# The load and store queue of a streaming encoder layer takes its order from the kernel's own planner

## The chip, the cores and the metric

The kernel runs on one core of a Trainium2 chip. The metric is the device time of one execution in microseconds (us). TensorE (PE in the profile) does the matmuls, VectorE (DVE), ScalarE (ACT) and GpSimd (POOL) the rest, and SyncE (SP) issues all DMAs.

## The reference, cut to what matters

One step of an encoder layer for 2048 new positions (prompt) and 64 further positions of a running stream (sample, with 4096 cached positions). All is float32.

```
h = rmsnorm(x, norm_g) @ w_in                  # 1024 -> 6144 columns
qa, ka, va, za, qb, kb, vb, zb, ga, gb = split(h)
# branch A: differential attention, 4 heads, two 64-wide halves c, 128-wide values
s = qa . ka / 8 - slope[h] * |q_pos - k_pos|,  masked by chunks of 64
a = softmax(s[c=0]) - lam * softmax(s[c=1]);   oa = a @ va
# branch B: retention with a running state r per head
s = (qb . kb) * d_intra;   ob = s @ vb + (qb * xi) @ r;   r = decay * r + (kb * zeta)^T @ vb
# output
oa = rmsnorm(oa) * silu(za);   ob = rmsnorm(ob) * silu(zb)
m = sigmoid(ga) * (oa @ w_oa) + sigmoid(gb) * (ob @ w_ob)
y = x + m @ w_out
```

The outputs are y, the normalised keys and values (k, v) of prompt and sample, and the retention states.

## The kernel before

Every large product is done as three matmuls on a high and a low part of each operand (hi*hi, hi*lo, lo*hi), so weights and inputs are split on ScalarE and on VectorE or GpSimd before they are used (`w_split`, `split_fin`).

The projection (`w_stream`) runs over the two halves of the prompt (1024 rows each, the sample with the first) and, within a half, over column groups of `w_in`. `natural` makes q, k, v and vb with rows on the partitions; `transposed` makes the others with columns on the partitions. A group's result leaves PSUM in a finishing task (`fin_qk`, `fin_va`, `fin_vb`, `fin_t`) that copies it to SBUF and stores it to scratch tensors in DRAM (`qT`, `kT`, `vN`, `vbN`, `qbT`, `kbT`, `zaT`, `zbT`, `gaT`, `gbT`). The buffers are few: one `thi`, two `tlo`, three `ev` (with `raw`).

The second stream (`z_stream`) runs beside it: for each half, attention over four heads. `load_head` fetches K and V of a head, `load_q` the queries of a pair of 128-row blocks, `qk_block` and `softmax` make the weights, `at_pv` multiplies with V and stores the normalised result to `oaT` from the one buffer `r_o`. After the first half come `sample_attn` and the retention (`ret_sample`, `ret_some`, `ret_block`), which stores to `obT`.

When the projection is done its pool is closed and the memory is used again for the output stage: `out_prep` loads w_oa and w_ob (`wst` in the buffers `oz`), o and z of each group of 264 columns, `load_wout` loads w_out, `gate` loads the gates (`gt`); `m_tile` and `m_fin` make m, `y_tile` and `y_fin` make y.

The order of the work comes from a planner inside the kernel. Each task is a Python generator; `loop` always advances the runnable task of the highest priority and emits its instructions as it goes. `P`, `A`, `V`, `G` add planned durations to clocks of the engines, `take` and `give` hand buffers out with the time at which they are believed free, and a `yield t` means "not before t on PE's clock". A DMA has a planned cost too:

```
    def ld(self, dst, src, nbytes=0):
        self.nc.sync.dma_start(dst, src)
        self.dma = max(self.dma, self.pe) + nbytes / 300.0
        return self.dma + DMA_LAT          # 2600 ns

    st = ld
```

The emitted order is binding only for the engines that `MANUAL` names: PE, ScalarE and VectorE. For SP and GpSimd the framework's scheduler chooses the order by its own estimate. All waits are semaphores that the framework derives from the data; an engine's queue works in order, so an instruction that waits holds back those behind it. Some loads are paced by the plan alone: x tiles by `XFLY` (three in flight in the first half, five in the second), the loads of a head until 9 us after the mark of its q, k and v.

Of the kernel before, what the change touches and what calls it, by code (L numbers as in the profile page):

```python
# [16 lines left out]
T = 2048  # L17
# [17 lines left out]
        "mm": 2, "s": 2, "at": 2, "pv": 1, "tp": 1,  # L35
        "oz": 11, "og": 16, "gt": 6, "wst": 4, "m": 18, "xt": 2, "yt": 2}
LAT = 250.0
DMA_LAT = 2600.0
QUANT = 6

# [16 lines left out]
class Hybrid:  # L57
# [449 lines left out]
    def fin_qk(self, which, g, nh=2):  # L507
        nc = self.nc
        ep = self.ep
        hs = slice(2 * g, 2 * g + nh)  # L510

        def fin(ps, r, nu, t0, t):
            n, ng, rt = 128 * nh * nu, 2 * nh * nu, r * nu
            yield from self.take("ev")
            yield from self.take("tlo")
            raw = self.sb(ep, [128, 512], "ev", "raw")[:r, :n]
            sq = self.sb(ep, [128, 512], "tlo", "sq")[:r, :n]
            ms = self.sp.tile([128, 8], F32, tag="ms", name="ms")[:r, :ng]
            raw3 = raw.rearrange("p (g d) -> p g d", d=64)
            nc.scalar.activation(sq, ps, AF.Square)  # L520
            t1 = self.A(n, t)
            if which == "q":
                nc.scalar.copy(raw, ps)
                t2 = self.A(n, t)
            else:
                nc.vector.tensor_mul(raw3, ps.rearrange("p (g d) -> p g d", d=64),
                                     self.gk[:r].unsqueeze(1).to_broadcast([r, ng, 64]))
                t2 = self.V(n, t)
            self.give("mm", max(t1, t2))
            yield t1  # L530
            nc.vector.tensor_reduce(ms, sq.rearrange("p (g d) -> p g d", d=64),
                                    axis=AX.X, op=ALU.add)
            t = self.V(n, t1)
            self.give("tlo", t)
            if which == "q":
                nc.vector.scalar_tensor_tensor(out=ms, in0=ms, scalar=64.0 * EPS,
                                               in1=self.qinv[:r, 2 if nh == 4 else g, :ng], op0=ALU.add, op1=ALU.mult)
            else:
                nc.vector.tensor_scalar(ms, ms, 1.0 / 64, EPS, op0=ALU.mult, op1=ALU.add)
            t = self.V(8)  # L540
            yield t
            rs = yield from self.rsqrt_small(ms, ng, t)
            nc.vector.tensor_mul(raw3, raw3, rs.unsqueeze(2).to_broadcast([r, ng, 64]))
            t = self.V(n)
            yield t
            ts = 0
            if which == "k":
                if t0 < T:
                    dst = self.o["k_prompt"][0, 0, t0:t0 + rt, hs]
                else:  # L550
                    dst = self.o["k_sample"][0, 0, :, hs]
                ts = self.rows_out(dst.rearrange("t h c d -> t (h c d)"), raw, nu, nh << 16)
            yield from self.take("tp")
            tp = self.psum("tp")
            for u in range(nu):
                for h in range(nh):
                    c = 128 * (nh * u + h)
                    nc.tensor.transpose(tp[:, h * rt + u * r:h * rt + u * r + r], raw[:, c:c + 128],
                                        self.ident[:r, :r])
                    t = self.P(256)  # L560
            self.give("ev", max(t, ts))
            yield from self.take("thi")
            yield from self.take("tlo")
            hi = self.sb(ep, [128, 512], "thi", dt=F32R)[:, :nh * rt]
            lo = self.sb(ep, [128, 512], "tlo", dt=F32R)[:, :nh * rt]
            pt = tp[:, :nh * rt]
            if which == "q":
                nc.scalar.activation(hi, pt, AF.Identity, scale=self.gq)
                nc.vector.scalar_tensor_tensor(out=lo, in0=pt, scalar=self.gq, in1=hi.bitcast(F32),
                                               op0=ALU.mult, op1=ALU.subtract)  # L570
                dst = self.qT
            else:
                nc.scalar.copy(hi, pt)
                nc.vector.tensor_sub(lo, pt, hi.bitcast(F32))
                dst = self.kT
            t1 = self.A(n, t, 40)
            t2 = self.V(n, t1)
            self.give("tp", t2)
            for d, s, tag, w in zip(dst, (hi, lo), ("thi", "tlo"), (t1, t2)):
                if w > self.pe:  # L580
                    yield w
                self.give(tag, self.st(d[hs, :, t0:t0 + rt].rearrange("h p t -> p h t"),
                                       s.bitcast(F32).rearrange("p (h t) -> p h t", h=nh), nh * nu << 16))

        return fin

    def fin_va(self, g, nh=2):
        nc = self.nc
        ep = self.ep
        hs = slice(2 * g, 2 * g + nh)  # L590

        def fin(ps, r, nu, t0, t):
            n, rt = 128 * nh * nu, r * nu
            yield from self.take("ev")
            yield from self.take("thi")
            yield from self.take("tlo")
            raw = self.sb(ep, [128, 512], "ev", "raw")[:r, :n]
            hi = self.sb(ep, [128, 512], "thi", dt=F32R)[:r, :n]
            lo = self.sb(ep, [128, 512], "tlo", dt=F32R)[:r, :n]
            nc.scalar.copy(hi, ps)  # L600
            t1 = self.A(n, t)
            nc.scalar.copy(raw, ps)
            t2 = self.A(n, t)
            nc.vector.tensor_sub(lo, ps, hi.bitcast(F32))  # L604
            t3 = self.V(n, t1)
            self.give("mm", max(t2, t3))
            if t0 < T:
                dst = self.o["v_prompt"][0, 0, t0:t0 + rt, hs]
            else:
                dst = self.o["v_sample"][0, 0, :, hs]  # L610
            yield t1
            gsl = slice(256 * g, 256 * g + 128 * nh)
            self.give("thi", self.rows_out(self.vN[0][t0:t0 + rt, gsl], hi.bitcast(F32), nu, nh << 16))
            yield t2
            td = self.rows_out(dst.rearrange("t h e -> t (h e)"), raw, nu, nh << 16)
            if t0 == T:
                td = self.st(self.vsN[:, gsl], raw, 1 << 16)
            self.give("ev", td)
            yield t3
            self.give("tlo", self.rows_out(self.vN[1][t0:t0 + rt, gsl], lo.bitcast(F32), nu, nh << 16))  # L620

        return fin

    def fin_vb(self, g):
        nc = self.nc
        ep = self.ep

        def fin(ps, r, nu, t0, t):
            n, rt = 256 * nu, r * nu
            yield from self.take("ev")  # L630
            raw = self.sb(ep, [128, 512], "ev", "raw")[:r, :n]
            nc.scalar.copy(raw, ps)
            t = self.A(n, t)
            self.give("mm", t)
            yield t
            self.give("ev", self.rows_out(self.vbN[t0:t0 + rt, 256 * g:256 * g + 256], raw, nu, 1 << 17))

        return fin
# [17 lines left out]
    def fin_t(self, ps, n, dst, t0, scale, grouped, t):  # L656
        nc = self.nc
        yield from self.take("ev")
        ev = self.sb(self.ep, [128, 512], "ev")[:, :n]
        if scale is None:  # L660
            nc.scalar.copy(ev, ps)  # L661
        else:
            nc.scalar.mul(ev, ps, scale)
        t = self.A(n, t)
        self.give("mm", t)
        yield t
        self.give("ev", self.put(dst, ev, t0, n, grouped))

    def put(self, dst, ev, t0, n, grouped):
# [233 lines left out]
    def at_pv(self, h, p, vs, tv, pair, last_pair):  # L903
# [26 lines left out]
        for kp in range(nkt // 2):  # L930
# [3 lines left out]
            w = 0  # L934
            segs = []
            for kt in (2 * kp, 2 * kp + 1):
                s0 = w
                for b in range(2):
# [4 lines left out]
                    t = self.P(256)  # L943
# [12 lines left out]
            t1 = self.A(w, t)  # L956
            nc.vector.tensor_sub(al[:, :w], at[:, :w], ah[:, :w].bitcast(F32))  # L957
            t2 = self.V(w, t1)
# [6 lines left out]
        t = done[0]  # L965
        if last_pair:
            self.give("V", t, len(vs[0]) * 2)
        o = yield from self.rms_t(pv, 256, self.gsub, t, "pv")
        self.give("r_o", self.put(self.oaT[h], o, 256 * p, 256, True))

    def sample_attn(self):
# [9 lines left out]
        for h in range(4):  # L981
# [3 lines left out]
            for j in range(2):  # L985
                nc.vector.memset(qq[j].bitcast(F32), 0.0)
                t = self.V(128)
# [35 lines left out]
            for m in range(9):  # L1023
                n = 512 if m < 8 else 64
                if m < 8:
                    yield lambda: len(self.kns) > 0
                    kn, t = self.kns.pop(0)
# [46 lines left out]
            t = self.P(512)  # L1074
        self.give("row", t, 2)
        o = yield from self.rms_t(fp, 256, self.gsub, t, "pv")
        for h in range(4):
            t = self.put(self.oaT[h], o[:, 64 * h:64 * h + 64], T, 64, True)
        self.give("r_o", t)
# [89 lines left out]
    def ret_block(self, k, t0, r, first):  # L1169
# [102 lines left out]
        nc.scalar.copy(res, tp)  # L1272
        t = self.A(4 * r, t)
        self.give("tp", t)
        yield t
        for h in range(4):
            rh = res[:, r * h:r * h + r]
            d3 = self.obT[h].rearrange("p (g c) -> p g c", c=GW)
# [244 lines left out]
    def y_fin(self, ps, xt, y, r, t):  # L1523
# [5 lines left out]
        t = self.V(512, t)  # L1529
        self.give("at", t)  # L1530
        self.give("xt", t)
        yield t
        self.give("yt", self.st(y, yt, 2048 * r))

    def out_stream(self):
# [138 lines left out]


def MANUAL(ET):
    return {ET.PE, ET.Activation, ET.DVE}


TLS = False  # L1680
# [60 lines left out]
```

## Time and profile before

| | |
|---|---|
| median of three runs | 2019.16 us (2017.9 to 2020.87) |
| the profiled execution | 2016.98 us, of which the span from first to last instruction 2015.2 us |
| mean granted TensorE clock | 0.997 |
| TensorE busy | 1991.4 us (99% of the span), 12414 matmuls |
| VectorE, ScalarE, GpSimd busy | 992.8, 956.9, 419.2 us |
| DMA | 278.8 MB on SP's queue, 46.8% of the time of the 16 DMA engines |

TensorE is the bound. The span is read in stages: to about 210 us only the projection runs; then projection and attention (or retention) share TensorE, with the second half's inputs transposed from about 810 us; the last group of the projection ends at about 1623 us and the output stage runs from there to the end. Waits of SP in the profile are times in which the head of its queue waits for a semaphore.

### The profile page before, as it was taken

Reading aid. Unit: us, or ns where it says so; the run is one execution under the profiler, and the core shown is the slowest. Engines: PE = TensorE matmul, PEld = TensorE weight load, DVE = VectorE, ACT = ScalarE, POOL = GpSimd, SP = SyncE. Lnnn points to the kernel's source line nnn. Section 1 sums busy time; section 2 is a strip of 40 time slices with the busy share of each in tenths; the row PEclk is TensorE's granted clock in tenths of the full one; section 3 lists DMA queues with packets and bytes.
Section 4 is the critical chain, followed back from the end, with each engine's and each line's share of the span. In section 5 each row is a group of like instructions: output and inputs, shape, how many; then the busy total and the mean of one; then the engine's idle time right before and its main releaser. Section 6 shows DMA issues by size and latency. Waiting matters only on the chain. (4 is left out here: it accounts for less than half of the span.)

```text
span 2015.2 us, 34341 instructions
## 1 busy us (share of the span) xinstructions
PE 1991.4 (99%) x12414; PEld 1786.1 (89%) x12414; DVE 992.8 (49%) x2659; ACT 956.9 (47%) x2096; POOL 419.2 (21%) x387
## 2 busy tenths in 40 slices
PE   8999999999999999999999999999999989999999
PEld 6778999999998999999999888888888878889997
DVE  6353575553331321546856655635653365444442
ACT  6332676654432433535666665645654544333221
POOL 2310121121112221221211111222112443222210
PEclk9999999999999999999999999999999999999999
DMA  6646464344565463563352252463234665444431
GB/s 228 195 146 171 135 168 130 101 140 144 150 182 131 135 178 104 164 198 123 112 157 87 85 158 68 124 190 95 64 92 126 202 216 159 144 146 133 140 94 58
DMA packets 330268, 280.96 MB, mean 139 GB/s; under 512 B 64689, under 2 KB 296113, under 8 KB 330098
## 3 DMA queue, kind: packets, MB, share of 16 engines
q1 hardware_dynamic: 330098, 278.77, 46.8%
q8 instruction: 98, 1.61, 0.3%
q14 instruction: 72, 0.59, 0.1%
HBM read 187.19 MB, written 91.49 MB: 138 GB/s over the span
## 5 line engine op out<-in xcount | busy, mean ns | idle before, releaser
L451 PE MATMUL mm<-xh,wh 128*128 128x512 f32 (+2 forms) x1280 | 461.1, 360 | 0.0
L451 PE MATMUL mm<-xh,wl 128*128 128x512 f32 (+2 forms) x1280 | 451.7, 353 | 0.0
L451 PE MATMUL mm<-xl,wh 128*128 128x512 f32 (+2 forms) x1280 | 450.9, 352 | 0.0
L422 POOL TENSOR_TENSOR wl<-ws,wh 128x512 fp32r<-128x512 f32 x190 | 251.9, 1338 | 912.3 <-ACT wh L415 632.2
L451 PE MATMUL mm<-wh,xh 128*128 128x256 f32 (+3 forms) x864 | 272.5, 315 | 0.3 <-DVE tlo L604 0.3
L451 PEld LDWEIGHTS mm<-xh,wl 128*128 128x128 f32 x1280 | 240.9, 188 | 31.9
L451 PEld LDWEIGHTS mm<-xh,wh 128*128 128x128 f32 x1280 | 241.2, 188 | 29.6 <-issue 0.2
L451 PEld LDWEIGHTS mm<-xl,wh 128*128 128x128 f32 x1280 | 241.5, 189 | 29.1
L451 PE MATMUL mm<-wh,xl 128*128 128x256 f32 (+3 forms) x864 | 267.2, 309 | 0.0
L451 PE MATMUL mm<-wl,xh 128*128 128x256 f32 (+3 forms) x864 | 266.9, 309 | 0.0
L661 ACT COPY ev<-mm 128x512 f32<-128x512 f32 x140 | 71.6, 511 | 238.8 <-PE mm L451 216.9
L451 PEld LDWEIGHTS mm<-wh,xh 128*128 128x128 f32 (+1 forms) x864 | 162.5, 188 | 11.0 <-PE s L836 0.4
L451 PEld LDWEIGHTS mm<-wl,xh 128*128 128x128 f32 (+1 forms) x864 | 162.7, 188 | 10.6
L451 PEld LDWEIGHTS mm<-wh,xl 128*128 128x128 f32 (+1 forms) x864 | 162.5, 188 | 10.2
L957 DVE TENSOR_TENSOR atl<-at,ath 128x512 fp32r<-128x512 f32 (+1 forms) x144 | 93.8, 660 | 139.8 <-ACT ath L955 139.8
L874 ACT ACTIVATE row<-row,a_mx 128x1024 f32<-128x1024 f32 (+7 forms) x160 | 153.6, 964 | 16.7 <-DVE a_mx L854 16.6
L844 DVE CUSTOM_DVE_ANT_0 row<-s,dfar 128x512 f32<-128x512 f32 (+2 forms) x192 | 117.9, 632 | 74.7 <-PE s L836 73.5
L415 ACT CAST wh<-ws 128x512 fp32r<-128x512 f32 x192 | 117.0, 619 | 40.7 <-PE mm L451 28.3
L955 ACT CAST ath<-at 128x512 fp32r<-128x512 f32 (+1 forms) x144 | 79.6, 563 | 99.3 <-PE at L942 96.9
L835 PE MATMUL s<-K,q 128*128 128x512 f32 (+3 forms) x320 | 120.3, 381 | 2.5 <-DVE a_acc L844 2.5
L836 PE MATMUL s<-K,q 128*128 128x512 f32 (+3 forms) x320 | 115.5, 362 | 0.7 <-DMA q<-qT 0.7
L895 DVE SCALAR_TENSOR_TENSOR row<-row,a_w 128x1024 f32<-128x1024 f32 (+4 forms) x96 | 98.1, 1032 | 26.7 <-ACT row L892 26.5
(206 smaller groups left out, 3945.5 us busy)
## 6 DMA issues: line engine op xcount, KB each, us to landing
ws<-in_w_in_dram SPq DMA_DIRECT2D x192, 256.0 KB, 3.1
q<-qT SPq DMA_DIRECT2D x128, 128.0 KB, 3.0
V<-vN SPq DMA_DIRECT2D x24, 512.0 KB, 5.5
K<-kT SPq DMA_DIRECT2D x48, 256.0 KB, 4.4
gt<-gaT SPq DMA_DIRECT2D x64, 132.0 KB, 2.1
gt<-gbT SPq DMA_DIRECT2D x64, 132.0 KB, 2.2
xt<-in_x_prompt_dram SPq DMA_DIRECT2D x16, 512.0 KB, 6.3
kn<-in_cache_k_T_dram SPq DMA_DIRECT2D x32, 256.0 KB, 3.9
```

The lines of the kernel that those rows point to most:

```text
L415: nc.scalar.copy(h, st)
L422: nc.gpsimd.tensor_sub(l, st, h.bitcast(F32))
L451: nc.tensor.matmul(ps, p, q, start=c == 0 and i == 0, stop=c == KC - 1 and i == 2)
L661: nc.scalar.copy(ev, ps)
L835: nc.tensor.matmul(ps, q1s, kk, start=True, stop=False)
L836: nc.tensor.matmul(ps, q2s, kk, start=False, stop=True)
L844: nc.vector.tensor_tensor_reduce(out=units[k0 // 1024][:, k0 % 1024:k0 % 1024 + n], in0=ps, in1=tab, scale=-SLOPES[h], scalar=3.0e38, op0= ...
L874: nc.scalar.activation(u, u, AF.Exp, bias=mx, scale=-1.0, accum_out=lp[:, k:k + 1])
L895: nc.vector.scalar_tensor_tensor(out=u0, in0=u0, scalar=w[:, 0:1], in1=u1, op0=ALU.mult, op1=ALU.add)
L955: nc.scalar.copy(ah[:, :w], at[:, :w])
L957: nc.vector.tensor_sub(al[:, :w], at[:, :w], ah[:, :w].bitcast(F32))
```

## The change

SP is added to the engines that follow the emitted order, so loads and stores go out in the order in which the planner emits them. Most stores are now emitted `STORE` = 700 ns after the planned time of their data (before: at that time), so that whatever the planner emits within these 700 ns stands ahead of them. In three places, `at_pv`, `sample_attn` and the k output in `fin_qk`, a store had followed its data at once: the first two now wait for the later of PE's and VectorE's planned clocks plus 700 ns, and the third stands behind the transposes of the same tile instead of ahead of them. The buffers of these stores are handed back by the planner with a correspondingly later time.

```
+STORE = 700.0
...
 def MANUAL(ET):
-    return {ET.PE, ET.Activation, ET.DVE}
+    return {ET.PE, ET.Activation, ET.DVE, ET.SP}
...
 # fin_qk: the k output moves from ahead of take("tp") to behind the transposes
-            ts = 0
-            if which == "k":
-                ...
-                ts = self.rows_out(dst.rearrange("t h c d -> t (h c d)"), raw, nu, nh << 16)
             yield from self.take("tp")
...
                     t = self.P(256)
+            ts = 0
+            if which == "k":
+                ...
+                ts = self.rows_out(dst.rearrange("t h c d -> t (h c d)"), raw, nu, nh << 16)
             self.give("ev", max(t, ts))
...
 # fin_qk, the hi and lo parts
-                if w > self.pe:
-                    yield w
+                if w + STORE > self.pe:
+                    yield w + STORE
...
 # fin_va: three stores;  fin_vb, fin_t, ret_block, y_fin: one wait each
-            yield t1
+            yield t1 + STORE
...
-            yield t2
+            yield t2 + STORE
...
-            yield t3
+            yield t3 + STORE
...
-        yield t
+        yield t + STORE
...
 # at_pv and sample_attn, ahead of the stores to oaT
         o = yield from self.rms_t(pv, 256, self.gsub, t, "pv")
+        yield max(self.pe, self.dve) + STORE
         self.give("r_o", self.put(self.oaT[h], o, 256 * p, 256, True))
```

More of the change, by code (lines that the diff above doesn't have):

```diff
@@ L545, in fin @@
             yield t
-            ts = 0
-            if which == "k":
[L548 to L551, printed above, removed]
-                ts = self.rows_out(dst.rearrange("t h c d -> t (h c d)"), raw, nu, nh << 16)
             yield from self.take("tp")
@@ L560, in fin @@
                     t = self.P(256)
+            ts = 0
+            if which == "k":
+                if t0 < T:
+                    dst = self.o["k_prompt"][0, 0, t0:t0 + rt, hs]
+                else:
+                    dst = self.o["k_sample"][0, 0, :, hs]
+                ts = self.rows_out(dst.rearrange("t h c d -> t (h c d)"), raw, nu, nh << 16)
             self.give("ev", max(t, ts))
@@ L665, in fin_t @@
         self.give("mm", t)
-        yield t
+        yield t + STORE
         self.give("ev", self.put(dst, ev, t0, n, grouped))
@@ L1076, in sample_attn @@
         o = yield from self.rms_t(fp, 256, self.gsub, t, "pv")
+        yield max(self.pe, self.dve) + STORE
         for h in range(4):
@@ L1274, in ret_block @@
         self.give("tp", t)
-        yield t
+        yield t + STORE
         for h in range(4):
@@ L1531, in y_fin @@
         self.give("xt", t)
-        yield t
+        yield t + STORE
         self.give("yt", self.st(y, yt, 2048 * r))
```

## The prediction

> **What bounds the kernel now.** I read the head of the page first, then the busy time by stretch, then who ended TensorE's waits, then the DMA queue's own waits and its order in time.
>
> ```profile
> span 2015.2 us, 34341 instructions
> PE 1991.4 (99%) x12414; PEld 1786.1 (89%) x12414; DVE 992.8 (49%) x2659; ACT 956.9 (47%) x2096; POOL 419.2 (21%) x387
> ```
>
> TensorE (PE) is busy for 1991.4 of 2015.2 us. Its 12414 matmuls are not touched, so only 2015.2 - 1991.4 = 23.8 us of idle time is open to an edit that reorders DMAs, plus whatever runs at a reduced clock. The next rows say where the idle time lies (first number after the stretch: its length; second: PE busy; the sixth field is the granted clock):
>
> ```profile
> 0.00:50.00 50.00, 44.37 (x198) 34.87 (x199) 31.14 (x70) 32.04 (x67) 11.99 (x13) 0.97 0.67 228
> 850.00:900.00 50.00, 49.13 (x412) 48.78 (x411) 26.85 (x59) 18.59 (x43) 10.27 (x8) 1.00 0.72 214
> 900.00:950.00 50.00, 48.91 (x375) 46.62 (x376) 29.12 (x87) 25.08 (x53) 5.14 (x4) 1.00 0.43 138
> 950.00:1000.00 50.00, 48.02 (x369) 45.97 (x368) 40.26 (x121) 33.91 (x73) 8.23 (x6) 1.00 0.31 95
> 1600.00:1650.00 50.00, 46.30 (x276) 41.71 (x275) 25.38 (x52) 21.36 (x51) 17.02 (x20) 0.97 0.61 187
> 1650.00:1700.00 50.00, 45.94 (x277) 40.74 (x277) 31.73 (x72) 20.41 (x52) 20.36 (x25) 0.97 0.59 185
> 2000.00:2016.00 16.00, 11.08 (x48) 6.21 (x46) 1.69 (x3) 0.00 (x0) 0.00 (x0) 0.99 0.23 67
> ```
>
> Idle: 5.63 us at the start, 0.87 + 1.09 + 1.98 = 3.94 us around the change of halves, 3.70 + 4.06 = 7.76 us at the switch to the output stage, 4.92 us at the very end. That is 22.25 of 23.8 us. Who ends PE's waits:
>
> ```profile
> PE at L1516 <- DVE ml L1485: 4.0, 2, 2.1
> PE tp L341 <- DVE xl L349: 3.9, 1, 3.9
> PE mm L1447 <- DVE gt L1467: 3.7, 3, 1.9
> PE s L835 <- DVE a_acc L844: 2.5, 4, 1.6
> PE tp L558 <- DVE raw L543: 1.3, 4, 0.5
> PE s L836 <- DMA q<-qT: 0.7, 1, 0.7
> ```
>
> Only one row, 0.7 us, is a load that the attention itself waits for. Everything else is VectorE being late. So the order of the loads can matter only through what makes VectorE late, and that is seen at one place, the switch at 1620 to 1665 us (chain of work, start and length of each piece):
>
> ```profile
> 1623.75 2.92 DMA gbT<-ev
> 1628.53 5.02 DMA wst<-in_w_out_dram
> 1633.58 0.63 ACT woh L1316
> 1634.23 0.69 DVE wol L1323
> ```
>
> The last store of the projection stage has to land before the output stage may reuse its memory; then w_out is loaded, split on ScalarE and VectorE, and VectorE, in program order, reaches its gate products (L1467) late. PE's waits of 3.7 and 4.0 us follow. They cost more than themselves, for the clock falls behind them:
>
> ```profile
> 1633.50:1637.00 3.50, 1.56 (x13) 1.35 (x12) 2.93 (x7) 3.25 (x7) 1.27 (x1) 0.99 1.04 386
> 1637.00:1640.30 3.30, 3.30 (x17) 3.30 (x16) 3.30 (x4) 2.43 (x6) 3.28 (x3) 0.50 0.43 131
> 1660.80:1664.20 3.40, 2.98 (x7) 2.42 (x8) 3.40 (x6) 1.02 (x3) 3.28 (x4) 0.50 0.54 165
> ```
>
> Two stretches of about 3.4 us run at a granted clock of 0.50, after a stretch with 1.56 us busy out of 3.50. Each costs about 1.7 us of work. The switch therefore holds 7.76 + 2 x 1.7 = 11.2 us.
>
> The Trainium skill (TensorE: Matmul & The Clock Gate, Part 1) says the clock halves after an idle window of about 3.4 us. The trace has the 3.4 us of half clock, but no wait of PE is that long (2.1 us at most), so here a window that is more than half idle was enough. By the page's rule, waits of about 2 us would bring no slow stretch, and the switch would hold 7.8 us; by the trace, such waits gathered in one window do.
>
> **The change, part by part.** No DMA, matmul or copy is added or removed. What moves is the order of SyncE's (SP's) queue, in which each issue holds back all behind it.
>
> *Where SP waits now.*
>
> ```profile
> SPq L132 <- POOL wl L422: 261.4, 152, 7.3
> SPq L132 <- ACT ev L661: 260.4, 85, 16.0
> SPq L132 <- DVE oyt L1528: 82.9, 23, 16.8
> ```
>
> ```profile
> 1618.32 0.38 SPq L132 DMA_DIRECT2D gbT<-ev  x1
> 1619.44 0.33 SPq L132 DMA_DIRECT2D z<-zaT  x1
> 1620.13 0.32 SPq L132 DMA_DIRECT2D on<-oaT  x1
> 1623.75 0.37 SPq L132 DMA_DIRECT2D gbT<-ev  x1
> 1624.52 0.94 SPq L132 DMA_DIRECT2D z<-zaT  x1
> 1627.59 3.93 SPq L132 DMA_DIRECT2D wst<-in_w_out_dram  x8
> ```
>
> SP stands 260.4 us in front of stores whose copy (L661) is not done, 3.1 us each time. From 1620.45 to 1623.75 it stands so with a z load behind it. Taking loads ahead of such stores is what the edit does. Its worth is bounded by what PE waits for: among PE's waits none is ended by `on` or `z`, and the 0.7 us for q is all a load delays directly. So from this part I take -0.7 us; at most the switch and the change of halves go too (rival 1).
>
> *The last gbT store at the switch.* The plan puts it 0.7 us (STORE) behind its data, and what follows it in the plan (closing the pool, w_out, the gates) moves too. On the chip SP does not wait for the plan's clock, only for order and semaphores: it reaches the store early and issues when the copy ends. Cost between 0 (SP is there first, as now) and 0.7 us plus one load in front that waits for its slot (3.1 us, the mean wait above). Nearest is the row at 1623.75, where SP waits for the store: I take 0, and keep +3.8 for the range.
>
> *The stores' later due times elsewhere.* Each due time also says when the planner believes a buffer is free, so with 0.7 us more the order on PE, ScalarE and VectorE can shift. The one buffer of `thi` is the tightest: in the plan it was held for the copy, two latencies of 0.25 us and a store of 262144/300 + 2600 ns, 0.6 + 0.5 + 3.5 = 4.6 us; now 5.3 us, against the 24 matmuls of a tile.
>
> ```profile
> 1589.79 0.39 PE L451 MATMUL mm<-xl,wh 128*128 128x512 f32 x1
> 1590.47 0.39 PE L451 MATMUL mm<-xl,wh 128*128 128x512 f32 x1
> ```
>
> These two stand three matmuls apart, 0.68/3 = 0.227 us each, so a tile takes 5.4 us. The hold still fits, with 0.1 us to spare; without that cover it would cost its excess in each tile. I take 0; either sign is possible, and I give it 4 us each way, the idle time around the change of halves (3.94), which is where such shifts now show.
>
> *Loads that stood far ahead fall back to their planned place.* The order of before runs ahead of the plan:
>
> ```profile
> 8.04 5.67 SPq L132 DMA_DIRECT2D xt<-in_x_prompt_dram  x6
> 33.87 0.43 SPq L132 DMA_DIRECT2D state<-in_state_ret_dram  x1
> ```
>
> Six x tiles are issued in a row though the plan allows three in flight (XFLY), and the retention state is fetched at 33.87 us, long before the sample's attention and the retention that follows it. Afterwards each stands where the plan has it, with the plan's latency, and that is shorter than the measured one:
>
> ```profile
> q<-qT SPq DMA_DIRECT2D x128, 128.0 KB, 3.0
> V<-vN SPq DMA_DIRECT2D x24, 512.0 KB, 5.5
> K<-kT SPq DMA_DIRECT2D x48, 256.0 KB, 4.4
> ```
>
> Plan for K: 262144/300 + 2600 ns = 3.47 us against 4.4, 0.9 late; for V 524288/300 + 2600 = 4.35 against 5.5, 1.15 late. If PE stood at each of the 8 heads for both: 8 x (0.9 + 1.15) = 16.4 us; if loads arrive before their turn, 0. The row nearest to this is q: its four loads per pair (planned 4 x 0.44 + 2.6 = 4.3 us, measured three issues more plus 3.0) are already fetched about as the plan has it, and 32 pairs cost PE 0.7 us in all. So I take 1 us and keep 16.4.
>
> [...]
>
> *The moved k store* (L548 to L552, now behind four transposes at most) is issued some tenths of a microsecond later and frees `ev` later; `ev` has three buffers, and no wait on it is among PE's rows. 0.
>
> *The end.*
>
> ```profile
> 2011.11 0.68 DVE oyt L1528
> ```
>
> The last store follows this addition with nothing else left in the queue, so its 0.7 us of planned delay is not waited for. 0.
>
> Sum: -0.7 + 0 + 0 + 1 + 0 + 0 = +0.3 us on the profiled execution, 2016.98 us (1.8 us around its span), giving 2017.3. That execution is 2.2 us below the median of 2019.16, so the median to expect is 2019.5 us.
>
> **The rivals.**
>
> *Rival 1, faster: the switch and the change of halves are relieved.* If loads no longer stand behind stores, w_out and the gates come earlier, VectorE's queue is not blocked, and the half-clock stretches vanish. Half of the switch (11.2/2 = 5.6) and half of the change of halves (3.94/2 = 2.0) give 2019.2 - 7.6 = 2011.6 us; all of both, and the 3.9 us of the start, would give 2000. For it: the 260.4 us of SP's waits. Against it: at the switch the chain begins with the store that was issued the moment its copy ended, and w_out's memory is not free before it lands; no order of the queue shortens that. The start's wait is VectorE's own order.
>
> *Rival 2, slower: K and V lose their lead.* Loads that no longer run ahead of the plan land after the time at which the plan sends PE to them: at a head's start PE stands until K or V is there. It decides once the plan's landing (3.47, 4.35 us) is the time at which PE is sent there with nothing placed between. Half of 16.4 us, and one half-clock stretch of 1.7 us, give 2019.2 + 9.9 = 2029.1 us; all of it with two stretches 2039. For it: the measured 4.4 and 5.5 us. Against it: q's 0.7 us, and that PE has projection matmuls to place between.
>
> *Rival 3, the change does not do what it says.* The old order may already be nearly the plan's: at the switch z, `on` and the gbT stores alternate as a plan would have them. Then the time is 2019.2 us. It can't be told from the forecast by time, only by the queue's order.
>
> **How the numbers follow.** Forecast and rival 3 together 0.42 (the forecast 0.32, rival 3 0.10), rival 1 0.25, rival 2 0.33; rival 2 is above rival 1 because its price has rows and rival 1's best place is held by a landing that stays. A measurement of this kernel can tell about 0.2% (4 us) from no change. The forecast's own range, with its 4 us each way and the 3.8, is 2014 to 2025, so of the 0.42 some 0.06 falls below 2015.2 and 0.07 above 2023.2: faster 0.25 + 0.06 = 0.31, same 0.29, slower 0.33 + 0.07 = 0.40. The range goes from 2009 (beyond rival 1's middle) to 2033 (beyond rival 2's).
>
> **What would show it.** Right: PE busy within 2 us of 1991.4, idle of 7 to 8 us between 1600 and 1700 with the same two slow stretches, SP's wait on L661 well below 260 us, state's load just ahead of the sample's retention. Rival 1 shows as granted clock 1.00 in those two stretches and less wait on L1467 and L1485. Rival 2 shows as new rows of PE waiting on DMA K or V, at the starts of heads. The prediction is wrong if PE's busy count or VectorE's waits change elsewhere, or if a store at the queue's head holds up a load that PE stands for.

## The result, and the profile after

The change makes the kernel slower: 2040.51 us median (2038.84 to 2041.96, four runs) against 2018.74 us (2017.9 to 2020.87, four runs), a ratio of 1.0112 with a 95% interval of 1.01 to 1.0123. The forecast of 2019.5 us and its range up to 2033 us missed it.

The head of the page after, with the chain that ended last:

```profile
span 2037.4 us, 34316 instructions
PE 1997.5 (98%) x12414; PEld 1792.1 (88%) x12414; DVE 990.6 (49%) x2659; ACT 959.7 (47%) x2096; POOL 420.3 (21%) x387
PE 91%; DVE 2%; DMA 2%; SPq 2%; issue 1%; ACT 1%; POOL 0%; POOLq 0%; ACTq 0%; DVEq 0%
```

The work is the same. Idle time of TensorE grew from 23.8 to 2037.4 - 1997.5 = 39.9 us, and the same 12414 matmuls are busy for 6.1 us more, at a lower granted clock. By stretch (length, PE busy, and the sixth field is the granted clock):

```profile
50.00:100.00 50.00, 46.94 (x211) 36.64 (x210) 17.28 (x56) 17.59 (x39) 17.20 (x13) 0.97 0.56 174
200.00:250.00 50.00, 47.60 (x360) 46.28 (x360) 21.95 (x87) 23.29 (x54) 5.82 (x5) 0.97 0.76 189
900.00:950.00 50.00, 37.54 (x261) 34.37 (x260) 15.04 (x44) 16.61 (x36) 8.18 (x7) 0.83 0.81 211
1600.00:1650.00 50.00, 50.00 (x242) 42.24 (x241) 19.81 (x35) 22.20 (x57) 19.50 (x21) 1.00 0.56 172
1650.00:1700.00 50.00, 42.52 (x240) 37.57 (x239) 39.64 (x73) 26.93 (x64) 25.39 (x28) 0.93 0.79 248
```

Three places are new. Around the change of halves (900 to 950 us) the idle time went from 1.09 to 12.46 us. At 50 to 100 us it went from nothing to 3.06, and at 200 to 250 us, where the first half's attention starts, from 0.70 to 2.40. In the kernel before these two stretches read:

```profile
50.00:100.00 50.00, 50.00 (x232) 39.62 (x231) 18.91 (x61) 19.49 (x43) 17.18 (x13) 1.00 0.62 198
200.00:250.00 50.00, 49.30 (x390) 48.00 (x389) 26.53 (x99) 29.57 (x67) 5.81 (x5) 1.00 0.54 141
```

The switch to the output stage is where it was, only later: 7.48 us idle and a clock of 0.93 over 50 us, against 7.76 us and 0.97 over 100 us.

Who ended TensorE's waits (total, times, longest, us), after:

```profile
PE s L836 <- DMA q<-qT: 13.3, 2, 11.5
PE mm L1450 <- DVE gt L1470: 5.2, 2, 3.4
PE mm L452 <- DVE tlo L605: 3.1, 1, 3.1
...
PE s L837 <- DMA q<-qT: 0.9, 2, 0.6
```

The rows on q are new in size: one wait of 11.5 us for a load of queries. SP's queue in time order (start, length of the whole group of issues) says why:

```profile
910.02 4.98 SPq L133 DMA_DIRECT2D K<-kT  x8
915.05 8.58 SPq L133 DMA_DIRECT2D V<-vN  x4
923.68 6.85 SPq L133 DMA_DIRECT2D q<-qT  x8
930.63 0.54 SPq L133 DMA_DIRECT2D vN<-thi  x1
```

At the second half's first head the planner emits eight K loads, four V loads and then q. That is 8 x 256 KB + 4 x 512 KB = 4 MB ahead of q in one queue, 923.68 - 910.02 = 13.7 us of issuing. The order of before had these twelve loads spread over some 300 us:

```profile
568.90 0.77 SPq L132 DMA_DIRECT2D K<-kT  x1
570.79 1.11 SPq L132 DMA_DIRECT2D K<-kT  x2
581.14 0.59 SPq L132 DMA_DIRECT2D K<-kT  x1
597.85 1.82 SPq L132 DMA_DIRECT2D V<-vN  x2
...
851.31 1.66 SPq L132 DMA_DIRECT2D V<-vN  x2
878.31 1.17 SPq L132 DMA_DIRECT2D K<-kT  x2
882.58 1.14 SPq L132 DMA_DIRECT2D K<-kT  x2
883.75 1.25 SPq L132 DMA_DIRECT2D q<-qT  x2
```

TensorE comes to its first product with this q at 919.5 us. For 4.2 us no q load has been issued; from the first one's issue at 923.68 us it takes another 7.3 us until the product starts at 930.98, against a median of 3.0 us from issue to landing. So q is late by its place in the queue and by the transfers under way ahead of it: in the stretches below the share of the DMA engines (the last field but one) is 1.09 and 1.20, so they have work all the time.

The wait is not paid once. The wait itself in two parts, and the stretch after it:

```profile
919.50:922.00 2.50, 0.00 (x1) 0.00 (x0) 0.00 (x0) 0.00 (x0) 0.00 (x0) 1.00 1.09 219
922.00:930.80 8.80, 0.00 (x0) 0.00 (x0) 0.00 (x0) 0.00 (x0) 0.00 (x0) 0.51 1.20 274
930.80:938.90 8.10, 7.41 (x19) 5.01 (x20) 4.06 (x15) 3.39 (x7) 0.00 (x0) 0.50 0.84 248
```

TensorE resumes at half clock and stays there for some 8 us, which loses about 4 us. This place holds 11.4 us more idle time and 4 us of clock, 15.4 us. The Trainium skill (TensorE: Matmul & The Clock Gate, Part 1) has the clock halve after an idle window of about 3.4 us, and this wait is such a one. But the clock is down about 2.7 us into it (1.00 up to 922.2 us, 0.50 from 922.5), so that the 3.4 us ahead of the fall held some 0.7 us of work: as in the profile of before, a window that is mostly idle was enough. The other two places add 3.06 us of idle time and 0.03 x 50 = 1.5 us of clock (50 to 100 us), and 1.7 and 1.5 us (200 to 250 us). All three come to 23.2 us, against 22.2 us of longer span. The first 50 us are left out of this: the granted clock there is 0.90 against 0.97 before, but the idle time is 0.7 us less, and by 50 us TensorE has done 113 of the matmuls of the projection against 106.

At 50 to 100 us the same thing happens with a store. Ten small constants, in eleven loads that take 7.1 us to issue, stand in a row, and a store of v behind them:

```profile
53.46 0.42 SPq L133 DMA_DIRECT2D fold<-in_c_fold_dram  x1
...
60.17 0.42 SPq L133 DMA_DIRECT2D lrow<-in_lam_k_dram  x1
60.70 0.36 SPq L133 DMA_DIRECT2D ws<-in_w_in_dram  x1
61.17 0.37 SPq L133 DMA_DIRECT2D vN<-thi  x1
```

The store empties the only `thi` buffer. ScalarE waits 8.18 us for it, VectorE's `tlo` (L605) follows, and TensorE waits 3.1 us for that. Before, these constants went out at 23 to 32 us, around the stores of v and not ahead of them.

### The profile page after: what moved, and what is told of

It is laid out like the page before. It is cut to its first block, busy times and chain, and to the rows that moved or that the text cites. A ratio compares the mean times of both kernels' runs of the same rounds, so it can differ in the third digit from the quotient of the medians.

```text
span 2037.4 us, 34316 instructions
## 1 busy us (share of the span) xinstructions
PE 1997.5 (98%) x12414; PEld 1792.1 (88%) x12414; DVE 990.6 (49%) x2659; ACT 959.7 (47%) x2096; POOL 420.3 (21%) x387
## 4 chain that ended last, share of the span: by engine, by line
PE 91%; DVE 2%; DMA 2%; SPq 2%; issue 1%; ACT 1%; POOL 0%; POOLq 0%; ACTq 0%; DVEq 0%
PE mm L452 50%; PE s L836 3%; PE s L837 3%; PE at L1517 3%; PE at L943 3%; PE at L1519 3%; PE at L1518 3%; SPq L133 2%; PE pv L923 2%; PE pv L922 2%; PE pv L921 2%; PE pv L1122 1%; PE mm L1450 1%; PE mm L1452 1%; PE mm L1451 1%; PE s L1451 1%
## 5 line engine op out<-in xcount | busy, mean ns | idle before, releaser
L662 ACT COPY ev<-mm 128x512 f32<-128x512 f32 x140 | 71.4, 510 | 224.5 <-PE mm L452 203.2
L836 PE MATMUL s<-K,q 128*128 128x512 f32 (+3 forms) x320 | 122.8, 388 | 14.7 <-DMA q<-qT 13.3
L837 PE MATMUL s<-K,q 128*128 128x512 f32 (+3 forms) x320 | 117.3, 368 | 0.9 <-DMA q<-qT 0.9
```

Of the source, the lines that this page charges most:

```text
L836: nc.tensor.matmul(ps, q1s, kk, start=True, stop=False)
L837: nc.tensor.matmul(ps, q2s, kk, start=False, stop=True)
```

## Experiments

Two theories were set against each other first. Theory Q: the order of SP's queue costs, because loads that had stood far ahead now go out in a burst and what the work needs first stands behind them. Theory P: the later due times (STORE) cost, because the planner's order on the other engines moves. Each ratio below is to the kernel before as it ran beside that experiment, with medians of 2017.94, 2019.04 and 2018.53 us.

**The plan alone.** SP goes back to the framework's order, all other edits stay.

```
-    return {ET.PE, ET.Activation, ET.DVE, ET.SP}
+    return {ET.PE, ET.Activation, ET.DVE}
```

> The changed kernel with SyncE given back to the framework's scheduler: the planner's 700 ns and the moved k store stay, only the queue's order is the old way. Theory Q (the loss is the queue: q behind K and V at the second half's first head, small constants ahead of a v store): about 2019 us, within 4 us of before, and no wait of TensorE on q over 2 us near 900 us. Theory P (the 700 ns shift the planner's order of TensorE, ScalarE and VectorE, and that is what costs): about 2040 us, as the changed kernel.

2016.34 us against 2017.94; ratio 0.9991 (0.9982 to 1.0001). The change of halves is as before (clock 1.00):

```profile
900.00:950.00 50.00, 48.91 (x376) 46.62 (x375) 29.54 (x87) 24.96 (x54) 6.03 (x4) 1.00 0.42 138
```

The whole loss goes with SP's order. P falls.

**The order alone.** SP stays in the planner's order.

```
-STORE = 700.0
+STORE = 0.0
```

> The changed kernel with STORE = 0: SyncE in the planner's order, stores at the planned time of their data. Theory Q: K, V and q of the second half's first head still go out in one block at the same planned time, so the wait of about 11 us on q stays; 2036 to 2046 us. Theory P: the plan is nearly that of before, so about 2019 us.

2039.01 us; 1.0108 (1.0093 to 1.0123). The wait on q is 12.8 us. The delay of the stores neither makes the loss nor relieves it.

**q ahead of K and V.** The task that loads q is spawned before the one that loads heads.

```
-            self.spawn(self.h_loader(half), 0, "z")
             self.spawn(self.q_loader(half), 0, "z")
+            self.spawn(self.h_loader(half), 0, "z")
```

> The changed kernel with the q loader spawned ahead of the K and V loader, so that at a head's start the eight q loads stand in front of the eight K and four V loads. Theory Q: q lands some 12 us earlier, K 5 us later; the wait at 919 us shrinks from 11.6 us to what K then sets, 0 to 3 us, and its half-clock stretch shrinks too: 2024 to 2031 us. Rival K (the burst of 4 MB is bandwidth bound and whatever stands last in it is waited for): the wait moves to K and stays over 8 us; 2036 to 2042 us.

2034.4 us; 1.008 (1.0065 to 1.0095), between the two ranges: less was won than Q expected. TensorE's waits in this run:

```profile
PE mm L452 <- DVE tlo L605: 6.5, 2, 3.3
PE s L836 <- DMA K<-kT: 5.8, 3, 3.7
```

The long wait on q is gone and two others have its place: K now stands behind q, and a store of v behind V (issued at 926.69 us), whose `thi` holds up `tlo`. Of the two rows, 4.2 us on K and 3.3 us on `tlo` fall at this place; the rest belongs to the places at 215 and 64 us. So it is not q's place alone but the burst: the loads and the store that stand behind its first part are late.

**The burst earlier.** K and V of a head are loaded 9 us after k is projected, not after q.

```
+        n0, n1 = (None, "kv0"), (None, "kv1")
...
-            yield from self.head_in(half, h)
+            k = f"kv{h // 2}{half}"
+            yield lambda: k in self.done
+            yield self.marks[k] + 9000
```

> The changed kernel with marks of their own for K and V: the loads of a head start 9 us after the mark of its k group instead of its q group, about 25 us earlier, as they did in the order of before. Theory Q: nothing stands ahead of q at 919 us, the wait there goes to under 2 us, and so does the one of 2 us at 215 us: 2020 to 2027 us. Rival K: some of the wait stays, as the transfers themselves are late: over 2032 us.

2031.97 us; 1.0072 (1.0057 to 1.0087), 5 us above Q's range and a hair under the rival's bound of 2032, so that the time alone decides nothing. The burst starts 17 us earlier, and weights for the projection come behind it, ahead of q:

```profile
893.20 4.98 SPq L133 DMA_DIRECT2D K<-kT  x8
898.22 8.36 SPq L133 DMA_DIRECT2D V<-vN  x4
906.69 3.06 SPq L133 DMA_DIRECT2D ws<-in_w_in_dram  x1
911.12 1.14 SPq L133 DMA_DIRECT2D ws<-in_w_in_dram  x2
912.31 6.45 SPq L133 DMA_DIRECT2D q<-qT  x8
```

TensorE still waits 8.4 us for q, so the wait is the rival's.

**V behind q.** For the first head of each half, V is loaded once the loads of two q have been emitted.

```
                 ks[c][u] = k
+        if h == 0:
+            yield lambda: len(self.qs) >= 2
```

> The changed kernel with the V loads of the first head of each half held back until its two q loads (eight DMAs) are out: order K, q, V. In the changed kernel V's four issues held SyncE for 8.6 us (915.05 to 923.68) ahead of q, K's eight for 5.0 us. Theory V (the blocked issues of V are most of the wait): the 11.6 us at 919 us become 2 to 4 us, and with less time at half clock the whole is 2026 to 2032 us. Rival K (4 MB of K and V are in flight and q waits for their transfer wherever it stands behind K): the wait stays over 8 us, 2035 us or more.

2035.21 us; 1.0085 (1.0068 to 1.0102). The time lies in the rival's range, but its wait of over 8 us is not there: the one on q fell to 4.2 us, about what theory V expected, and one of 2.9 us on `tlo` came behind it, for V now stands ahead of the store of v.

**The constants apart.** At eight places among the loads of the constants the planner is made to wait 1.2 us.

```
         self.ld(self.fold, i["c_fold"])
+        yield self.pe + 1200
         self.rzeta = c("rzeta", [128, 8])
         self.ld(self.rzeta, i["c_rzeta"])
+        yield self.pe + 1200
...
```

> The changed kernel with the small constant loads (fold, rzeta, gq, gk, bg, gsub, lambda) set 1.2 us apart in the plan, so that the v stores get in between. Theory C (the 3.2 us wait at 64 us, and its half-clock stretch, come from the ten constant loads that stand in SyncE's queue ahead of the store that frees thi): the wait goes, 2034 to 2037.5 us. Rival: the store is late for another reason (w_in loads ahead of it): the wait stays, 2039 to 2042 us.

2033.73 us; 1.0077 (1.0062 to 1.0092), 0.3 us under the range of theory C. The place at 64 us is relieved, and the wait on q stays (10.8 us):

```profile
50.00:100.00 50.00, 49.04 (x226) 38.56 (x225) 19.99 (x61) 18.32 (x41) 14.61 (x12) 1.00 0.62 188
900.00:950.00 50.00, 38.27 (x264) 34.88 (x263) 15.53 (x50) 17.21 (x36) 6.16 (x5) 0.83 0.83 218
```

**Half of the burst early.** The K and V of the first 1024 keys of the second half's first head, which the first half's projection has already stored, are loaded as soon as the first half's attention hands out its buffers; they have 3 us of plan between them.

```
+    def pre_head(self):
+        for c in range(2):
+            yield from self.take("K")
+            ...
+            yield self.pe + 3000
...
+            if half == 1:
+                self.spawn(self.pre_head(), 0, "z")
```

> The changed kernel with the part of the second half's first head that belongs to the first 1024 keys (two K tiles, two V tiles, 2 MB) loaded before the mark, as the order of before had it by some 300 us. What is left at the mark, ahead of q: four K and two V loads. Theory Q: the wait at 919 us falls from 11.6 to 2 to 5 us; 2026 to 2033 us. Rival K (transfer bound): over 8 us stay, 2035 us or more.

2031.42 us; 1.0064 (1.0047 to 1.0082). The burst in front of q is halved, and the wait on q falls from 11.5 to 2.8 us:

```profile
900.00:950.00 50.00, 46.17 (x323) 42.65 (x323) 22.21 (x63) 19.27 (x41) 8.62 (x7) 0.90 0.72 199
```

**These three together** (V behind q, constants apart, half of the burst early).

> The three edits together. Theory Q says that the three places are what the change lost: 22 us less 15 (at 919 us), 5 (at 64 us) and up to 3 (at 215 us): 2016 to 2021 us, no slower than before. If something else is still hidden in the order: 2025 us or more.

2022.43 us; 1.0021 (1.0012 to 1.0031), 1.4 us above the expected range. Some 18 of the 22 us are back; 3.4 us are still lost, and the interval is clear of 1.

```profile
900.00:950.00 50.00, 46.77 (x333) 42.88 (x333) 29.52 (x83) 24.27 (x52) 6.92 (x6) 0.97 0.70 192
```

No long wait on a DMA is left here. The idle time is still 3.23 us against 1.09 before, in short waits on VectorE, and one stretch of 3.4 us at half clock is left. That rest was not taken apart further.

**The lead taken away in the old order.** The kernel before, with the framework's order on SP, but the slots of K and V are held until 9 us after the mark, so that the first head's loads can't be early. No line of the change is in it.

```
+            if half == 1:
+                held = []
+                for tag, n in (("K", 4), ("V", 4)):
+                    yield from self.take(tag, n)
+                    held += [self.sb(self.ap, [128, 1024], tag, "hold") for _ in range(n)]
+                for k in held:
+                    nc.vector.memset(k[:, 0:1], 0.0)
...
+                yield from self.head_in(1, 0)
+                ...
+                self.give("K", t, 4)
+                self.give("V", t, 4)
```

> The kernel before, with its old SyncE queue, but the slots of K and V are held until 9 us after the last K, Q and V projection group of the second half's first heads, so that this head's K and V loads of the first 1024 keys lose their lead; 8 one-element memsets on VectorE are added twice to hold and free them. Theory (the lost lead is what costs, whatever scheduler writes the queue): K and V, 4 MB, now stand behind each other at about 920 us in the old order too; as in the runs with q first and with V last, the wait moves to K or to VectorE's tlo and stays about 4 to 11 us with half clock behind it: 2024 to 2036 us. Rival (the other differences of the two orders cost, the lead does not): within 3 us of the kernel before, 2016 to 2021 us.

2026.38 us; 1.004 (1.0024 to 1.0055), in the range of the theory: 7.9 us lost, with SP's order still the framework's. The framework's scheduler writes the same burst when it is not allowed to go ahead, and a store of v is what stands behind it:

```profile
902.05 4.95 SPq L132 DMA_DIRECT2D K<-kT  x8
907.10 8.21 SPq L132 DMA_DIRECT2D V<-vN  x4
915.40 1.69 SPq L132 DMA_DIRECT2D vN<-thi  x1
```

```profile
PE mm L451 <- DVE tlo L604: 7.8, 1, 7.8
```

So the lead is what the old order was worth at this place. It costs less here than in the change; two q had been fetched at 882.75 and 889.67 us, ahead of the burst, which can account for the difference but was not tried apart.

**Two tries at the switch.** The plan counts w_out's loads with 512 KB where 256 KB move, so that VectorE's splits of it come later in its queue: once without SP in the planner's order, once with the three mends.

```
-                t = self.ld(s, self.i["w_out"][0, 128 * ct:128 * ct + 128, sl], 1 << 18)
+                t = self.ld(s, self.i["w_out"][0, 128 * ct:128 * ct + 128, sl], 1 << 19)
```

> The change without SyncE's order (the run at 2016.3 us), and the plan counts w_out's eight loads with 512 KB each where 256 KB are moved, so that VectorE's splits of w_out (wol) stand later in its queue. If VectorE's queue blocked by the late w_out is what makes the switch to the output stage hold 7.8 us of idle time and two stretches at half clock: 2010 to 2014 us, with granted clock 1.00 at 1637 and at 1660 us. If the store, the load and the split themselves set it: 2015 to 2018 us, or slower, with the idle time and the half clock as before.

2019.19 us; 1.0001 (0.9993 to 1.001). No gain. TensorE's waits at the switch in this run:

```profile
PE mm L1450 <- DVE gt L1470: 6.6, 3, 4.1
...
PE at L1517 <- ACT mh L1480: 2.2, 1, 2.2
```

The wait on the gates grew from 4.6 us in the run of the plan alone, and that on `ml` (2.9 us there) became one on `mh`. The edit did part of what it was for: the first split of w_out keeps its place in VectorE's queue and the next ones move back, and VectorE's own waits for w_out's high part between 1600 and 1700 us fall from 3.7 us in the run of the plan alone to 0.8. TensorE gains nothing from that. That VectorE's queue, blocked by the split of w_out, is the cost of the switch is not borne out; that the first split alone blocks it is not excluded.

> The change with the three mends together (the run at 2022.4 us), and the plan counts w_out's loads with 512 KB each. If VectorE's blocked queue is the cost of the switch: 4 to 8 us less than 2022.4, so 2014 to 2018 us. If not: 2020 to 2024 us.

2026.68 us; 1.0037 (1.0024 to 1.0049). That is above the range for either outcome, and no gain again. It is 4.2 us more than without the edit, but the two intervals overlap, so that slower is not shown.

The best of the runs is the plan without SP's order (2016.34 us), and its interval does not part it from the kernel before.

## Why the prediction was wrong

**The step that failed** is "Loads that stood far ahead fall back to their planned place", taken at 1 us and kept at 16.4. It measured about 22 us, the whole loss (by the sum above 15.4 us at the change of halves, 4.6 at the constants and 3.2 at the first half's first head), and its working was wrong in kind too. I priced the lost lead by latency, 0.9 us for each K and 1.15 us for each V, at each of eight heads. The two rows on q hold four waits, all at the first head of a half; at the other six heads no load is waited for. At the second half's first head it is 11.5 us, for the place in the queue: 13.7 us of issues, and 4 MB, ahead of q. My bound was a latency, about 1 us for each load; what set the wait was everything that stands ahead in the queue. The rows to see it were there. In the timeline of before, K and V of this head go out up to some 340 us ahead of their use at 912.6 us, and `load_head` and `load_q` become runnable at the same mark, K and V first.

**"The row nearest to this is q"** was the wrong neighbour. Its 0.7 us in 32 pairs is what q costs when nothing stands ahead of it in the queue. It says nothing of q behind 4 MB. The same holds for "the order of the loads can matter only through what makes VectorE late": that TensorE waited for no other load was what the old order had brought about, and no sign that the order does not matter.

**Rival 2** named the mechanism, a lost lead, and the direction, with a chance of 0.33. It expected waits on K or V at the starts of heads; the wait is on q, at the first head of a half, and only the run with q first has K's row. Its upper figure, 2039 us, is near the measured 2040.5 us, but by another sum.

**The constants** were not in the sum at all. I listed x tiles and the state as loads that run ahead, and not the ten small ones that now stand between weights and a store.

**What held.** The later due times and the moved k output were taken at 0, and the plan alone is within the error of the kernel before (0.9991); the order alone costs the same with and without the 0.7 us. The switch kept its idle time (7.76 before, 7.48 us after) and its two stretches of half clock, as the forecast said, and rival 1 fell there: in the planner's order too its chain begins with the store of gbT (2.28 us) and the load of w_out (6.48 us). The state's load went from 33.87 to 647.4 us, just ahead of the sample's retention.

**Two signs did not come true.** TensorE's busy time was to stay within 2 us of 1991.4 and came to 1997.5, by the half clock behind the new waits. And SP's wait on L661 (now L662) was to fall well below 260 us:

```profile
SPq L133 <- POOL wl L423: 277.5, 130, 8.8
SPq L133 <- ACT ev L662: 251.1, 73, 15.9
```

The 0.7 us behind the data hardly change how long SP stands in front of stores. Rival 3, that the order hardly changes, is excluded by the same timelines.

## What to carry to other kernels

Before taking over a queue's order, list for each load how far ahead of its use the old order has it; a planner that issues loads when they are due must be given that lead as a task of its own, or the loads come out in one burst. Price such a burst by the time that its issues take, by how late a load lands behind it and by whatever else stands behind it, loads and stores alike, and not by the latency of one load. A queue that shows no waits on loads may owe that to its order. Reordering within the burst won 5 to 6 us here and moved the rest of the wait to the next in line; loading half of it early won 9.

## What the runs showed of the hardware

An issue can be held up, and it holds up all behind it. In the chain of work after, these are the issues of the four V loads of the burst, 512 KB each (start and length, all of it SP's own queue):

```profile
915.05 0.59 SPq L133
915.68 0.58 SPq L133
916.30 5.52 SPq L133
921.87 1.76 SPq L133
```

The eight K issues ahead of them take up to 0.60 us each, which is no more than usual: in the kernel before the median is 0.57 us for a K load, 0.60 for a q load and 0.37 for one of w_in. So ten issues, 3 MB, go out smoothly, and the eleventh holds the queue for 5.52 us. The timeline names nothing that it waits for.

Neither the number of issues ahead nor their bytes alone sets this. With q first it is again the third V that is held, for 5.56 us, behind 18 issues and 4 MB; with half of the burst early it is the q behind two V, for 3.11 us, behind six issues and 2 MB. Each time it is what stands right behind two V loads. The kernel fetches V in rows of 512 bytes and K in rows of 4096; whether the number of such pieces holds SP up was not tried.

A wait of 3.1 us is enough to bring the clock down. The one at 64 us was followed by

```profile
67.60:68.90 1.30, 1.30 (x6) 1.08 (x7) 0.00 (x0) 0.00 (x0) 0.00 (x0) 1.00 1.03 388
68.90:72.30 3.40, 3.40 (x10) 2.62 (x9) 1.74 (x11) 1.28 (x3) 0.00 (x0) 0.50 0.70 261
```

The half clock comes 1.3 us after TensorE has resumed and lasts 3.4 us, as long as each of the two stretches that the prediction shows in the kernel before, which came after several shorter waits. The wait of 11.5 us kept the clock at 0.50 from 922.2 to 939.3 us, about 8 us of it after work had resumed.
